# A transformer layer in emulated fp32: a fifth pair of k tiles in seven units, a fixed VectorE order at the start, and other banks for one projection

## The chip, the cores and the metric

The kernel runs on one core of one Trainium2 chip. The metric is the device time of one execution in microseconds (us). Engines: PE is TensorE (matmuls), DVE is VectorE, ACT is ScalarE, POOL is GpSimd, SP is SyncE, which here only issues DMAs.

## The reference

One layer on 256 tokens of 2048 channels. The parts that matter here are its matrix products with weights from HBM:

```python
z = u @ w_in                       # 2048 -> hq hf hi hg aq ak av, gates (2 x 2048)
o = hgrn2_scan(...)                # from hq, hf, hi; chunks of 64
ya = chunk_band_attention(...)     # from aq, ak, av
merged = gate_a * (y_a @ w_branch_a) + gate_b * (y_b @ w_branch_b)
h = h + merged @ w_out
h = h + square(relu(rms_norm(h) @ w_up)) @ w_down      # 2048 -> 8192 -> 2048
return rms_norm(h, norm_final_w)
```

All data are fp32.

## The kernel before, in words

**Three products for one.** Every fp32 operand is split into a high part, rounded to the matmul's faster format, and the rest. A split of weights is one cast on ACT (wh, L91) and one subtraction on DVE (wl, L92). A product is three matmuls: high by wh, high by wl, low by wh (L139, L140, L141 inside mm3). The activations (act_x, act_h, act_u) are split as they are made. A piece of weights is a raw tile of 128 x 1024: two k tiles of 128 rows by 512 columns. It is loaded by SP's queue (L215), and its two parts lie in the buffers wh and wl. There are four of each in the pool wpool, and from gb0 on a fifth one, which takes every fifth piece (buf, L201).

**The start.** After 12 warm-up matmuls (L81) the projections hf0 and hq0 run side by side, k tile by k tile, with x itself scaled and split on the way (L279 to L282; `xw` is x as loaded). They form their products transposed (L181 with wh, L186 with wl), two 256-token sums in a bank of their own each. Then hf1, then hq1. The banks of ps_acc are four; hf0 and hq0 hold them all, and add_parts (L195) adds their parts into f and zq.

**Units.** From av on, most products run as units of 256 tokens x 1024 columns x 16 k tiles. k tiles 0 to 3 and 4 to 7 with the two column halves make a 2 x 2 block matrix (A, B over D, C); it is multiplied in Strassen's way, in the form of Winograd, with 7 block products where 8 are usual. The sums of weights for it are formed in place: A += B and A += C on DVE (L846), B += C and D += A by accumulating DMAs that POOL issues (L851). The combinations of activations (S2, S4, S5, S7) are formed once per activation in combos. k tiles 8 to 15 are multiplied plainly. The block products are 11A, 22A, 12C, 11D, 21A, 21B, 21D, named after the bank they add to and the weight tile; each has two pieces of six matmuls a bank. A plain piece (`r` in the names) has two k tiles, 12 matmuls.

The order in a unit (run, L887): 11A; a late item of the unit before; 22A; another late item; 12C and 11D (11D first if there is no late item and the unit isn't spread); plain; 21A; plain; 21B; plain; plain; 21D; plain; plain; and the unit's own two last plain pieces are the late items of the next. "Spread" units are ga and gb; in them A += C comes after the subtractions of both 12C and 11D. All splits and sums have a raised priority; a scheduler puts each engine's instructions in order, and `issue_after` pins one behind another. Small work of the unit before (copies of y, L1211; gates, L729; evictions) is spread between the splits on ACT.

Units in order, with their start in us in the trace: av 245, qk 290, ga0 337, ga2 384, gb0 432, gb2 468, (branches by gemm2 514,) wo0 604, wo2 640, up00 683, up02 726, dn00 768, dn02 811, up10 852, up12 893, dn10 936, dn12 978, up20 1019, up22 1060, dn20 1103, dn22 1145, up30 1186, up32 1227, dn30 1270, dn32 1313 to 1359. upNM is columns of quarter N of the MLP's inner width, dnNM its way back.

**Loads.** The next unit's A is loaded during 21A, its B and C after 21B, its D after 21D, all on SP's queue, in the pools raw (6 tiles), rawd (2) and rawp (3).

Of the kernel before, what the change touches and what calls it, by code (L numbers as in the profile page):

```python
# [16 lines left out]
P = 128  # L17
# [33 lines left out]
def tile_hybrid_block(  # L51
# [26 lines left out]
    with tc.high_priority(offset=10000):  # L78
        nc.vector.memset(warm, 0.0)
        for _ in range(12):  # L80
            nc.tensor.matmul(ps_warm, warm, warm, start=True, stop=True)  # L81
# [6 lines left out]
    casts, marks, newest = [], [], []  # L88

    def split(hi, lo, src, copy=None):  # L90
        casts[:] = [(copy or nc.scalar.copy)(hi, src)]  # L91
        return nc.vector.tensor_tensor(lo, src, hi.bitcast(F32), op=ALU.subtract)  # L92
# [127 lines left out]
    def parts(raw, what):  # L220
# [9 lines left out]
        return [t.rearrange("p (a n) -> p a n", a=2) for t in made]  # L230

# [20 lines left out]
    def h2(what, bufs=10):  # L252
# [5 lines left out]
          weights(w_in_t, C_HQ, KD, T, "hq0", (1, 1) + (2,) * 7, beside=4)]  # L258
# [12 lines left out]
    for kt, n in zip(starts, steps):  # L271
# [3 lines left out]
        with tc.high_priority(offset=2000):  # L275
            for j in range(n):
# [3 lines left out]
                else:  # L280
                    nc.scalar.activation(hi, xw[:, j, :], AF.Copy, scale=g)
# [76 lines left out]
    acc_f1 = gemm_t(xT, w_in_t, C_HF + T, KD, "hf1")  # L358
# [376 lines left out]
    def combos(lhs, what, home, made, blocks=None):  # L735
# [11 lines left out]
        def final(i, s):  # L747
            t = home.tile([P, 4, 2, P], F32R, name=f"S{i}_{what}", tag=f"S{i}", bufs=1)
# [17 lines left out]

    def evict(dst, acc):
# [5 lines left out]

    class Unit:


        def __init__(self, lhs, S, w, n0, what, done, kt0=0, apart=NC, steps=lambda: (), start=5, fresh=None, held=False, tail=False):
# [4 lines left out]
            self.raw, self.dma, self.c, self.items, self.steps = {}, {}, {}, list(ITEMS), []  # L782

        def load(self, name):
# [3 lines left out]
                              for g in (0, 2)]  # L788

# [97 lines left out]
    def run(u, then=None):  # L887
# [18 lines left out]
        if not late and not u.spread:  # L906
# [24 lines left out]
        u.plain(1, (8, 9))  # L931
# [10 lines left out]
        u.plain(1, (10, 11))  # L942
# [15 lines left out]
        u.plain(0, (10, 11))  # L958
# [30 lines left out]
        late.append(lambda: u.plain(1, LATE[0]))  # L989
# [4 lines left out]
    for f in combos(xT, "x", tk, Sx):  # L994
# [50 lines left out]
    for m in range(NM):  # L1045
        scaled("k0", rstd, m, acc_k[m])
# [270 lines left out]
```

## Time and profile before

| | |
|---|---|
| median of 3 runs | 1369.27 us (1367.44 to 1372.15) |
| the profiled execution | 1368.19 us, span 1366.5 us |
| granted TensorE clock, mean | 0.999 |
| busy: PE, DVE, ACT, POOL | 99%, 82%, 69%, 11% of the span |
| DMA | 333.75 MB, mean 244 GB/s |

A line of the timeline gives start, duration, engine, line of the code, operation, tile written, tiles read, and in brackets the idle time of the engine before it with what released it. "PE acc_up10c" is a bank of unit up10, "wl_up10p11D" the low part for its product 11D, "wl_up10r" that of a plain piece. Matmuls overlap: one of 512 columns shows 0.39 us, and the next starts sooner. The durations below come from the one profiled execution.

### The profile page before, as it was taken

The numbers are of one execution on the slowest core, as the hardware profiler recorded it, in microseconds if no ns is written. First come the engines' busy times: TensorE is split into PE (matmuls) and PEld (weight loads), VectorE is DVE, ScalarE is ACT, GpSimd is POOL, SyncE is SP. The second block draws the span as 40 slices with busy tenths as digits, with TensorE's granted clock in tenths as the row PEclk, the third lists the DMA queues.
The fourth block names the chain that finished last, engine by engine and source line by source line (L and its number), as shares of the span: only waits on it lengthen the run. The fifth ranks groups of instructions, "written<-read, shape, count | busy, mean of one in ns | idle before, by whom it ended". The sixth has DMA issues, their size and how long they took to land.

```text
span 1366.5 us, 19044 instructions
## 1 busy us (share of the span) xinstructions
PE 1356.7 (99%) x6791; PEld 1123.1 (82%) x6791; DVE 1122.1 (82%) x1302; ACT 948.6 (69%) x1247; POOL 150.5 (11%) x231
## 2 busy tenths in 40 slices
PE   9999999999999999999999999999999999999997
PEld 7888888878778888888888888888888888888886
DVE  7888977887787775798998987789787888878886
ACT  6877765776777664455778766687666876668864
POOL 4000000111111000010121112100111002110210
PEclk9999999999999999999999999999999999999999
DMA  9754557788886986669899889988899888998892
GB/s 324 246 186 157 178 179 265 217 219 246 261 222 169 295 293 208 184 155 317 290 263 284 222 260 298 297 242 228 263 279 301 253 246 240 282 299 258 259 280 105
DMA packets 128895, 333.75 MB, mean 244 GB/s; under 512 B 11152, under 2 KB 12176, under 8 KB 128416
## 3 DMA queue, kind: packets, MB, share of 16 engines
q1 hardware_dynamic: 107936, 265.59, 56.4%
q0 software_dynamic: 20144, 66.14, 24.7%
q8 instruction: 53, 0.87, 0.3%
q10 hardware_dynamic: 720, 0.81, 0.2%
q14 instruction: 42, 0.34, 0.1%
HBM read 271.67 MB, written 10.49 MB: 206 GB/s over the span
## 4 chain that ended last, share of the span: by engine, by line
PE 98%; DMA 1%; ACT 0%; DVE 0%; issue 0%; SPq 0%; POOLq 0%; POOL 0%; ACTq 0%; DVEq 0%
PE acc_hf L181 2%; PE acc_hq L181 2%; PE tp_u L109 1%; PE acc_hg L139 1%; PE acc_qkc L139 1%; PE acc_hg L141 1%; PE acc_ba L141 1%; PE acc_hi L140 1%; PE acc_hi L139 1%; PE acc_bb L139 1%; PE acc_hi L141 1%; PE acc_hg L140 1%; PE acc_bb L141 1%; PE acc_ba L140 1%; PE acc_bb L140 1%; PE acc_ba L139 1%
## 5 line engine op out<-in xcount | busy, mean ns | idle before, releaser
L181 PE MATMUL acc_hf<-act_x,wh_hf 128*128 128x512 f32 x128 | 40.6, 399 | 0.4 <-DVE f L195 0.4
L181 PE MATMUL acc_hq<-act_x,wh_hq 128*128 128x512 f32 x128 | 40.5, 398 | 0.0
L91 ACT CAST wh_bb<-raw_bb 128x1024 fp32r<-128x1024 f32 x16 | 16.9, 1054 | 23.3 <-PE acc_ba L141 17.5
L92 DVE TENSOR_TENSOR wl_bb<-raw_bb,wh_bb 128x1024 fp32r<-128x1024 f32 x16 | 19.6, 1224 | 14.8 <-ACT wh_bb L91 14.7
L91 ACT CAST wh_ba<-raw_ba 128x1024 fp32r<-128x1024 f32 x16 | 16.8, 1053 | 19.9 <-PE acc_bb L141 13.8
L92 DVE TENSOR_TENSOR wl_ba<-raw_ba,wh_ba 128x1024 fp32r<-128x1024 f32 x16 | 19.6, 1223 | 10.8 <-ACT wh_ba L91 10.8
L186 PEld LDWEIGHTS acc_hq<-act_x,wl_hq 128*128 128x128 f32 x128 | 23.4, 188 | 6.1 <-DVE wl_hq L92 0.9
L186 PEld LDWEIGHTS acc_hf<-act_x,wl_hf 128*128 128x128 f32 x128 | 23.4, 188 | 6.0 <-DVE wl_hf L92 0.9
L1212 POOL DMA_DIRECT2D hd<-y x24 | 26.2, 1156 | 1.8 <-ACT y L1211 1.3
L92 DVE TENSOR_TENSOR wl_hf<-raw_hf,wh_hf 128x1024 fp32r<-128x1024 f32 (+2 forms) x21 | 20.3, 968 | 6.7 <-ACT wh_hf L91 6.7
L92 DVE TENSOR_TENSOR act_u<-tp_u,act_u 128x512 fp32r<-128x512 f32 x32 | 21.9, 685 | 4.7 <-ACT act_u L91 4.2
L139 PE MATMUL acc_bb<-wh_bb,act_yb 128*128 128x512 f32 x64 | 25.2, 393 | 0.0
L186 PE MATMUL acc_hq<-act_x,wl_hq 128*128 128x256 f32 x128 | 24.7, 280 | 0.4 <-DVE wl_hq L92 0.4
L186 PE MATMUL acc_hf<-act_x,wl_hf 128*128 128x256 f32 x128 | 24.7, 279 | 0.4 <-DVE wl_hf L92 0.4
L139 PE MATMUL acc_hg<-wh_hg,act_x 128*128 128x512 f32 x64 | 25.1, 392 | 0.0
L139 PE MATMUL acc_hi<-wh_hi,act_x 128*128 128x512 f32 x64 | 25.0, 391 | 0.0
L141 PE MATMUL acc_hg<-wh_hg,act_x 128*128 128x512 f32 x64 | 24.9, 390 | 0.0
L141 PE MATMUL acc_ba<-wh_ba,act_ya 128*128 128x512 f32 x64 | 24.9, 389 | 0.0
L141 PE MATMUL acc_hi<-wh_hi,act_x 128*128 128x512 f32 x64 | 24.9, 389 | 0.0
L140 PE MATMUL acc_hi<-wl_hi,act_x 128*128 128x512 f32 x64 | 24.9, 389 | 0.0
L140 PE MATMUL acc_hg<-wl_hg,act_x 128*128 128x512 f32 x64 | 24.9, 389 | 0.0
L139 PE MATMUL acc_ba<-wh_ba,act_ya 128*128 128x512 f32 x64 | 24.9, 389 | 0.0
(1996 smaller groups left out, 5226.6 us busy)
## 6 DMA issues: line engine op xcount, KB each, us to landing
raw_hi<-in_w_in_n_dram SPq DMA_DIRECT2D x16, 512.0 KB, 4.2
raw_hg<-in_w_in_n_dram SPq DMA_DIRECT2D x16, 512.0 KB, 4.3
raw_ba<-in_w_branch_a_dram SPq DMA_DIRECT2D x16, 512.0 KB, 4.6
raw_bb<-in_w_branch_b_dram SPq DMA_DIRECT2D x16, 512.0 KB, 4.7
raw_hf<-in_w_in_t_dram SPq DMA_DIRECT2D x12, 512.0 KB, 4.5
raw_hq<-in_w_in_t_dram SPq DMA_DIRECT2D x12, 512.0 KB, 5.5
hd<-y POOLq DMA_DIRECT2D x24, 256.0 KB, 7.4
raw_aq<-in_w_in_t_dram SPq DMA_DIRECT2D x8, 512.0 KB, 3.8
```

The source lines that it names most:

```text
L91: casts[:] = [(copy or nc.scalar.copy)(hi, src)]
L92: return nc.vector.tensor_tensor(lo, src, hi.bitcast(F32), op=ALU.subtract)
L109: nc.tensor.transpose(tp[:, j, :], src[:, j * P:(j + 1) * P], ident)
L139: nc.tensor.matmul(acc, hi, wh, start=first, stop=False, skip_group_check=True)
L140: nc.tensor.matmul(acc, hi, wl, start=False, stop=False, skip_group_check=True)
L141: newest[:] = [nc.tensor.matmul(acc, lo, wh, start=False, stop=last, skip_group_check=True)]
L181: newest[:] = [nc.tensor.matmul(acc[cb], wh[:, cb * P:(cb + 1) * P], r.rearrange("p u t -> p (u t)"), start=kt == 0, stop=last)]
L186: newest[:] = [nc.tensor.matmul(acc[cb][:, 0:T], wl[:, cb * P:(cb + 1) * P], r[:, 0, :], start=False, stop=False)]
L1212: nc.gpsimd.dma_start(hd[n][m], t, accum_op=ALU.add)
```

## The change

**A fifth pair.** Seven units (gb2, dn02, up10, dn12, up20, dn22, up30) also take k tile 8 with k tile 9 into the 7 products. Their weights are two more tiles, X (columns of A and D: k tile 8 is A's, 9 is D's) and Y (B's and C's), each with one buffer, loaded in the place of a plain piece each. Each product gets a third piece, a half: 512 columns, with its own cast, subtraction and buffer, and 3 matmuls. Four sums of 512 columns a unit are formed in X and Y on DVE (L862 in the new numbering). Two plain pieces go, and the unit has one late item instead of two. So the units behind a five unit have one late item in them; the rule for "11D first" is now "fewer than two late items", which holds in up10, up12 and so on. A += C is pinned behind the first of the two middle products. `fifths` forms the fifth part of the combinations of x (in gb0), h (in dn02) and u (in dn00, dn10, dn20).

**Room for it.** The fifth buffer of wh and wl is gone, everywhere. S7 is written into the place of one block of the activation that is never used otherwise; so the split of that block is left out for h and u. For x, which the plain projections read whole, S7 is formed only after ak.

**The start.** Ten warm-ups for 12; the DVE order is pinned; the third load of hq moves from ACT's queue to SP's; hf1's sums lie in the two banks of ps_sm.

By the printed order the matmul rows of PE go from 5997 to 5976, DVE's rows from 1278 to 1368, ACT's from 1169 to 1203.

The core of the diff:

```diff
-        for _ in range(12):
+        for _ in range(10):
...
-    def gemm_t(rhs, w, n0, nkt, what):
-        acc = new_acc(what)
+    def gemm_t(rhs, w, n0, nkt, what, acc=None):
+        acc = acc or new_acc(what)
...
-        if "fifth" in homes:
-            taken[tag] += 1
-        last = taken[tag] > 0 and taken[tag] % 5 == 0
-        return (homes["fifth"] if last else wpool).tile([P, 2 * NC], F32R, name=f"{tag}_{what}", tag=tag, bufs=1 if last else 4)
+        return wpool.tile([P, 2 * NC], F32R, name=f"{tag}_{what}", tag=tag, bufs=4)
...
+    def half(raw, a, what):
+        made = [buf(t, what)[:, 0:NC] for t in ("wh", "wl")]
+        with tc.high_priority(offset=2000):
+            lows.append(split(*[t.rearrange("p (c n) -> p c n", n=T) for t in made], view5(raw, a)))
+        return made
...
-          weights(w_in_t, C_HQ, KD, T, "hq0", (1, 1) + (2,) * 7, beside=4)]
+          weights(w_in_t, C_HQ, KD, T, "hq0", (1, 1) + (2,) * 7, beside=2)]
...
+            if kt in (1, 2):
+                es.enter_context(tc.issue_after(low[0].ins))
...
-    acc_f1 = gemm_t(xT, w_in_t, C_HF + T, KD, "hf1")
+    acc_f1 = gemm_t(xT, w_in_t, C_HF + T, KD, "hf1", [ps_sm.tile([P, NC], F32, name=f"acc_hf1{j}", tag="sm") for j in range(2)])
...
+    ITEMS5 = [(1, (10, 11)), (1, (12, 13)), (0, (10, 11)), (0, (12, 13)), (0, (14, 15)), (1, (14, 15))]
+    FIFTH = {"A": ("X", 0), "D": ("X", 1), "B": ("Y", 0), "C": ("Y", 1)}
+    SUMS5 = {("22", "A"): "B", ("21", "A"): "C", ("21", "B"): "C", ("21", "D"): "A"}
...
+                if not g and self.five and (i, name) in SUMS5:
+                    dst, src = [view5(self.raw[r], a) for r, a in (FIFTH[name], FIFTH[SUMS5[i, name]])]
+                    with tc.issue_after(lows[-1].ins), tc.high_priority(offset=2000):
+                        nc.vector.tensor_tensor(dst, dst, src, op=ALU.add)
...
+            if self.five:
+                raw, a = FIFTH[name]
+                mm3(self.c[i], *left(4), *half(self.raw[raw], a, f"{self.what}p{i}{name}5"), False, False)
...
-        if not late and not u.spread:
+        if len(late) < 2 and not u.spread:
             seconds.reverse()
...
         seconds[0]()
+        behind_first = lows[-1]
...
-            if u.spread:
-                es.enter_context(tc.issue_after(lows[-1].ins))
+            if u.spread or u.five:
+                es.enter_context(tc.issue_after((lows[-1] if u.spread else behind_first).ins))
             u.sums("A", "C")
...
             then.load("D")
+            then.load5("X")
...
-        late.append(lambda: u.plain(1, LATE[0]))
+        if not u.five:
+            late.append(lambda: u.plain(1, LATE[0]))
         late.append(rest)
```

**What moves on DVE at the start.** Before; act_x is the scaled x, lm and e are small vectors that are needed later:

```order
L279 TENSOR_SCALAR act_x_107<-xw_140,vt 128x256
L92 TENSOR_TENSOR wl_hf_0_122<-raw_hf_0_120,wh_hf_0_121 128x256
L282 SCALAR_TENSOR_TENSOR act_x_107<-xw_140,vt,act_x_107 128x256
L91 CAST wh_hf_0_121<-raw_hf_0_120 128x256
L307 TENSOR_TENSOR e_375<-vt,lm 128x8
L92 TENSOR_TENSOR wl_hf_0_122<-raw_hf_0_120,wh_hf_0_121 128x256
L92 TENSOR_TENSOR wl_hq_0_132<-raw_hq_0_130,wh_hq_0_131 128x256 x2
```

And after:

```order
L92 TENSOR_TENSOR wl_hf_0_120<-raw_hf_0_118,wh_hf_0_119 128x256
L92 TENSOR_TENSOR wl_hq_0_130<-raw_hq_0_128,wh_hq_0_129 128x256
L291 TENSOR_SCALAR act_x_105<-xw_138,vt 128x256
L294 SCALAR_TENSOR_TENSOR act_x_105<-xw_138,vt,act_x_105 128x256
L91 CAST wh_hf_0_119<-raw_hf_0_118 128x256
L92 TENSOR_TENSOR wl_hf_0_120<-raw_hf_0_118,wh_hf_0_119 128x256
L92 TENSOR_TENSOR wl_hq_0_130<-raw_hq_0_128,wh_hq_0_129 128x256
```

The low parts of the first pieces of hf and hq now come ahead of x's second k tile, and e has left this stretch.

**What moves on DVE in up10, from 22A to the first plain piece.** Before; `raw_up10A<-raw_up10A,raw_up10C` is A += C:

```order
L846 TENSOR_TENSOR raw_up10A_7831<-raw_up10A_7831,raw_up10C_7880 128x1024
L92 TENSOR_TENSOR wl_up10p22A_8044<-raw_up10A_7833,wh_up10p22A_8043 128x1024
L92 TENSOR_TENSOR wl_dn02r_14_8056<-rawp_dn02r_14_7901,wh_dn02r_14_8055 128x1024
L846 TENSOR_TENSOR raw_up10A_7833<-raw_up10A_7833,raw_up10C_7882 128x1024
L92 TENSOR_TENSOR wl_up10p12C_8080<-raw_up10C_7880,wh_up10p12C_8079 128x1024
L92 TENSOR_TENSOR wl_up10p12C_8090<-raw_up10C_7882,wh_up10p12C_8089 128x1024
L92 TENSOR_TENSOR wl_up10p11D_8100<-rawd_up10D_7939,wh_up10p11D_8099 128x1024
L92 TENSOR_TENSOR wl_up10p11D_8110<-rawd_up10D_7941,wh_up10p11D_8109 128x1024
L92 TENSOR_TENSOR wl_up10r_8_8124<-rawp_up10r_8_7975,wh_up10r_8_8123 128x1024
```

And after:

```order
L92 TENSOR_TENSOR wl_up10p11D_8161<-rawd_up10D_8019,wh_up10p11D_8160 128x1024
L92 TENSOR_TENSOR wl_up10p11D_8171<-rawd_up10D_8021,wh_up10p11D_8170 128x1024
L92 TENSOR_TENSOR wl_up10p11D_8181<-rawx_up10X,wh_up10p11D_8180 128x512
L898 TENSOR_TENSOR raw_up10A_7913<-raw_up10A_7913,raw_up10C_7968 128x1024
L92 TENSOR_TENSOR wl_up10p12C_8188<-raw_up10C_7968,wh_up10p12C_8187 128x1024
L92 TENSOR_TENSOR wl_up10p12C_8198<-raw_up10C_7970,wh_up10p12C_8197 128x1024
L92 TENSOR_TENSOR wl_up10p12C_8208<-rawy_up10Y,wh_up10p12C_8207 128x512
L898 TENSOR_TENSOR raw_up10A_7915<-raw_up10A_7915,raw_up10C_7970 128x1024
L92 TENSOR_TENSOR wl_up10r_10_8219<-rawp_up10r_10_8057,wh_up10r_10_8218 128x1024
```

11D now comes ahead of 12C, each has a half behind it, and the two sums of A stand between 11D and the first plain piece, where they stood among 22A's splits.

**What moves on SP's queue at the end of dn02.** After; X and Y are the new loads, and the plain pieces of up10 stand behind X:

```order
L211 DMA rawy_up10Y<-in_w_up_dram 128x2x512
L211 DMA rawp_dn02r_14_7871<-in_w_down_dram 128x1024
L211 DMA rawd_up10D_8019<-in_w_up_dram 128x2x512
L211 DMA rawd_up10D_8021<-in_w_up_dram 128x2x512
L211 DMA rawx_up10X<-in_w_up_dram 128x2x512
L211 DMA rawp_up10r_10_8057<-in_w_up_dram 128x2x512
```

The load of Y has come in behind C's, and X stands between D's two loads and those of the plain pieces.

More of the change, by code (lines that the diff above doesn't have):

```diff
@@ L930, in run @@
         u.step(next(at))
-        u.plain(1, (8, 9))
+        u.plain(1, (10, 11) if u.five else (8, 9))
         item(u)
@@ L941, in run @@
         u.step(next(at))
-        u.plain(1, (10, 11))
+        u.plain(1, (12, 13) if u.five else (10, 11))
         u.less("12", u1)
@@ L951, in run @@
             then.load("C")
+            then.load5("Y")
         u.step(next(at))
-        u.plain(0, (8, 9))
+        u.plain(0, (10, 11) if u.five else (8, 9))
         u.less("22", u2)
@@ L957, in run @@
         u.step(next(at))
-        u.plain(0, (10, 11))
+        if not u.five:
+            u.plain(0, (10, 11))
         u.residual("11")
@@ L987, in rest @@
             u.end(1)
-        late.append(lambda: u.plain(1, LATE[0]))
+        if not u.five:
+            late.append(lambda: u.plain(1, LATE[0]))
         late.append(rest)
     Sx = {}
-    for f in combos(xT, "x", tk, Sx):
+    x_sums = combos(xT, "x", tk, Sx)
+    for f in x_sums[:3]:
         f()
@@ L1046, in tile_hybrid_block @@
         scaled("k0", rstd, m, acc_k[m])
+    x_sums[3]()
     yb += [new_act(f"yb{g}") for g in range(2)]
@@ L1204, in tile_hybrid_block @@
             units.append(Unit(lambda: hT, lambda: Sh, w_up, qd * (FF // NQ) + c * NC, f"up{qd}{c}", done,
-                              steps=(lambda turns=turns: turns(0)) if c else (lambda: ()) if qd else (lambda: h_blocks(2)), start=3 if c else 0, held=not qd and not c))
+                              steps=(lambda turns=turns: turns(0)) if c else (lambda: ()) if qd else (lambda: h_blocks(2)), start=3 if c else 0, held=not qd and not c, five=qd > 0 and not c))
         def out_of(m, n, acc, c=slice(0, NC), last=last, qd=qd):
@@ L1267, in tile_hybrid_block @@
                               lambda m, n, acc, *c, n0=n0, out_of=out_of: out_of(m, n0 + n, acc, *c), kt0=qd * KD,
-                              steps=(lambda: ()) if n0 else (lambda turns=turns, last=last: turns(2) + [(3, finals)] * last),
-                              start=0, tail=last and n0 == 2))
+                              steps=(lambda qd=qd: [(99, lambda: fifths(hT, "h", sp, Sh))] * (not qd)) if n0 else (lambda turns=turns, last=last: turns(2) + [(3, finals)] * last),
+                              start=3 if n0 else 0, tail=last and n0 == 2, five=n0 == 2 and not last))
     for u, then in zip(units, units[1:] + [None]):
```

78 lines of the change are left out of this document (57 added, 21 removed).

## The prediction

> **What bounds the kernel now.** I read the page first: the busy times (part 1) and the chain of work that ended last (part 4).
>
> ```profile
> span 1366.5 us, 19044 instructions
> ...
> PE 1356.7 (99%) x6791; PEld 1123.1 (82%) x6791; DVE 1122.1 (82%) x1302; ACT 948.6 (69%) x1247; POOL 150.5 (11%) x231
> ...
> PE 98%; DMA 1%; ACT 0%; DVE 0%; issue 0%; SPq 0%; POOLq 0%; POOL 0%; ACTq 0%; DVEq 0%
> ```
>
> TensorE (PE) is busy 99% of the span and is 98% of the chain. So a matmul that goes is worth its own time, and any new wait of PE costs its own time. Next the waits of PE; the columns are total us, times, longest us.
>
> ```profile
> PE ps_warm L81 <- DVE warm L79: 1.1, 1, 1.1
> PE acc_hf L186 <- DVE wl_hf L92: 0.4, 1, 0.4
> PE acc_hq L186 <- DVE wl_hq L92: 0.4, 1, 0.4
> PE acc_hf L181 <- DVE f L195: 0.4, 1, 0.4
> ```
>
> These are all its waits, and all lie in the first 31 us. Three of the four are touched by the change; from there on PE never waits. The third view cuts the span at the units (gb2, up00, dn02, up10):
>
> ```profile
> core 0: us, PE busy (x) PEld busy (x) DVE busy (x) ACT busy (x) POOL busy (x), PEclk, DMA share, GB/s
> 467.80:513.80 46.00, 46.00 (x204) 38.09 (x203) 32.30 (x29) 30.29 (x34) 2.11 (x3) 1.00 0.85 268
> 682.90:725.60 42.70, 42.70 (x198) 35.35 (x197) 40.86 (x44) 31.22 (x41) 8.46 (x11) 1.00 0.93 276
> 811.10:851.90 40.80, 40.80 (x181) 33.80 (x180) 32.26 (x29) 26.96 (x30) 6.94 (x9) 1.00 0.98 283
> 851.90:892.70 40.80, 40.80 (x181) 33.79 (x180) 32.36 (x29) 27.60 (x31) 6.93 (x9) 1.00 1.00 284
> ```
>
> In up10 VectorE (DVE) works 32.4 of 40.8 us, in up00 already 40.9 of 42.7. The weights' DMA share in up10 is 1.00. So a unit has some 8 us of DVE to spare where the change adds work, and no DMA to spare.
>
> **What is removed: matmuls.** The timeline of PE gives the price of one.
>
> ```profile
> 857.35 0.39 PE L139 MATMUL acc_up10c<-wh_up10p22A,S_h 128*128 128x512 f32 x1
> ...
> 860.07 0.39 PE L139 MATMUL acc_dn02c<-wh_dn02r,act_u 128*128 128x512 f32 x1
> ```
>
> Between these two starts lie the 12 matmuls of product 22A: 2.72 us, 0.227 us each. A unit has 7 products x 4 tiles x 3 plus 8 plain k tiles x 4 x 3 = 180; with a fifth pair 7 x 5 x 3 + 6 x 4 x 3 = 177. Seven units lose 3 each: 21 x 0.227 = **4.77 us**. Nothing hides this, since PE is the chain.
>
> **The start.** PE, DVE and ScalarE (ACT) before:
>
> ```profile
> 1.12 4.77 PE L81 MATMUL ps_warm<-warm 128*128 128x128 f32 x24 [1.12 <-DVE warm L79]
> 5.65 0.71 PE L181 MATMUL acc_hf<-act_x,wh_hf 128*128 128x512 f32 x2
> 6.81 0.50 PE L186 MATMUL acc_hf<-act_x,wl_hf 128*128 128x256 f32 x2 [0.45 <-DVE wl_hf L92]
> ...
> 8.57 0.63 PE L181 MATMUL acc_hf<-act_x,wh_hf 128*128 128x512 f32 x2
> 9.04 0.40 PE L186 MATMUL acc_hf<-act_x,wl_hf 128*128 128x256 f32 x2
> ...
> 9.97 0.63 PE L181 MATMUL acc_hf<-act_x,wh_hf 128*128 128x512 f32 x2
> ```
> ```profile
> 5.83 0.55 DVE L279 TENSOR_SCALAR act_x<-xw,vt 128x256 fp32r<-128x256 f32 x1 [0.52 <-DMA xw<-in_x_t_dram]
> 6.31 0.45 DVE L92 TENSOR_TENSOR wl_hf<-raw_hf,wh_hf 128x256 fp32r<-128x256 f32 x1
> ...
> 9.31 0.69 DVE L92 TENSOR_TENSOR wl_hf<-raw_hf,wh_hf 128x512 fp32r<-128x512 f32 x1 [0.28 <-ACT wh_hf L91]
> ```
> ```profile
> 8.00 0.51 ACT L281 ACTIVATE act_x<-xw,vt 128x256 fp32r<-128x256 f32 x1 [1.56 <-DMA xw<-in_x_t_dram]
> 8.66 0.62 ACT L91 CAST wh_hf<-raw_hf 128x512 fp32r<-128x512 f32 x1
> ```
>
> DVE waits for a load of x (5.83) with wl_hf queued behind it (6.31), and PE waits for wl_hf. The new order puts wl_hf and wl_hq ahead. Both PE waits of 0.45 go, and two warm-ups fewer let the first real matmul come earlier. What is late next is k tile 2: its x comes from a DMA at 8.00, its cast ends at 9.28, and it starts at 9.97. So at most 9.97 - 9.28 = 0.69 us can come back, and at least nothing; the third hq load, moved from ACT's queue into SP's, stands ahead of later loads of x there and can take some 0.4 us (one issue, below). I take **0.4**, range -0.3 to 0.69. The Trainium skill ("TensorE: Matmul & The Clock Gate", Part 1: The HAM clock gate) says the array's clock opens only after a free-running window of about 3.4 us of activity, so ten warm-ups may end before it opens in some runs; an estimate by that page is up to 1 us of half-rate matmuls, which would turn this term into -0.6. No run here shows ten warm-ups; in the units shown above the granted clock was 1.00.
>
> **What is removed: the wait of hf1.**
>
> ```profile
> 29.01 0.63 PE L181 MATMUL acc_hq<-act_x,wh_hq 128*128 128x512 f32 x2
> 30.05 0.83 PE L181 MATMUL acc_hf<-act_x,wh_hf 128*128 128x512 f32 x2 [0.41 <-DVE f L195]
> ```
> ```profile
> 28.44 1.23 DVE L92 TENSOR_TENSOR wl_hf<-raw_hf,wh_hf 128x1024 fp32r<-128x1024 f32 x1 [0.69 <-ACT wh_hf L91]
> 29.58 0.75 DVE L195 TENSOR_TENSOR f<-acc_hf,f 128x256 f32<-128x256 f32 x2
> ```
>
> hf1 waits until the sums of hf0 have left their banks (f, L195). In other banks it need not. After a pair of such matmuls the next group starts 0.47 us on (8.57 to 9.04 above), so hf1 could start at 29.48: 0.57 us earlier. Its first pair also lasts 0.83 where others last 0.63. I take 0.57 and some 0.12 of the latter, **0.69** (0.57 to 0.77). The split at 28.44 is already hf1's second, so its first piece is ready, and nothing is late next: f is wanted again only when hf1's banks have taken all its pieces. So the gains are 4.77 + 0.4 + 0.69 = **5.86 us**.
>
> **What is added: splits and sums on DVE and ACT, with one buffer fewer.** Prices:
>
> ```profile
> L92 DVE TENSOR_TENSOR wl_up10r<-rawp_up10r,wh_up10r 128x1024 fp32r<-128x1024 f32 x7 | 8.6, 1224 | 4.2 <-ACT wh_up10r L91 3.9
> ```
> ```profile
> 478.96 2.36 DVE L846 TENSOR_TENSOR raw_gb2A<-raw_gb2A,raw_gb2C 128x1024 f32<-128x1024 f32 x2
> 481.23 1.22 DVE L92 TENSOR_TENSOR wl_gb2r<-rawp_gb2r,wh_gb2r 128x1024 fp32r<-128x1024 f32 x1
> ```
>
> A 1024-column operation lasts 1.22 us on DVE and follows the one before after 1.14 (2.27 for two); a 512-column one lasts 0.69 (9.31 above), in a row, by the same difference, some 0.6. Per unit two plain splits go (-2.4) and seven half splits and four sums of 512 come (+7.5): 32.4 + 5.1 = 37.5 of 40.1 us. ACT gains seven casts of 0.62 and loses two of 1.05: 27.6 + 2.2 = 29.8. On the average both still fit under PE. dn02 also forms h's fifth combinations (two operations of 512, four of 128 columns; about 2 us by these rows, less than 2.8): some 39.5 of 40.1. What decides is how far splits may run ahead. There were five buffers for wh and wl, now there are four, and a half piece fills one too. A split may start when the piece four places before it has been used. The av unit before gb0 already has four:
>
> ```profile
> 249.07 0.39 PE L139 MATMUL acc_avc<-wh_avp22A,S_x 128*128 128x512 f32 x1
> ```
> ```profile
> 249.35 1.05 ACT L91 CAST wh_avp12C<-raw_avC 128x1024 fp32r<-128x1024 f32 x1
> ```
>
> PE leaves the first 22A piece at 249.07, and the cast four places on starts 0.28 later. The subtraction starts 1.08 after its cast and lasts 1.22:
>
> ```profile
> 857.59 1.05 ACT L91 CAST wh_up10p12C<-raw_up10C 128x1024 fp32r<-128x1024 f32 x1 [1.23 <-issue]
> ```
> ```profile
> 858.67 1.22 DVE L92 TENSOR_TENSOR wl_up10p12C<-raw_up10C,wh_up10p12C 128x1024 fp32r<-128x1024 f32 x1 [0.36 <-ACT wh_up10p12C L91]
> ```
>
> That is 2.6 us from release to use. Three pieces in hand are 4.08 us of PE when full, but two full ones and a half are 3.40, plus 0.23 to the first matmul that reads wl: 1.0 us of slack, if DVE is free at that moment. A sum of 1.14 ahead of the split takes it all.
>
> **up10, up20, up30.** PE's order (pieces of 1.36, halves 0.68, late piece 2.72): 11A to 3.40, late 6.12, 22A 9.52, 11D 12.92, 12C 16.32, then the first plain piece. 11D's first buffer is released at 6.12, ACT has there two copies of y:
>
> ```profile
> 861.75 0.59 ACT L1211 COPY y<-acc_dn02c 128x512 f32<-128x512 f32 x1
> ```
>
> I put its cast at 6.85 and its subtraction at 7.93. From there DVE has 11D (1.14 + 1.14 + 0.60), a sum of A (1.14), 12C (2.28 + 0.60), a sum of A (1.14) and the plain split (1.22): 9.26, to 17.19. PE wants that at 16.32 + 0.23 = 16.55. So PE waits about 0.65; without the copies ahead 0, with the first copy at the release 1.4. Queued behind the late split on DVE is product 21A, whose slack is the plain piece's 2.72. 3 x 0.65 = **1.95** (0 to 4.3).
>
> **gb2** has both sums in a row ahead of the plain split, and two late pieces: 12C begins at 12.24, 11D at 15.64, plain at 19.04. 11D's buffer comes free at 12.24, behind a gate on ACT
>
> ```profile
> 478.91 0.69 ACT L729 ACTIVATE gate_gb<-acc_gb0c,rstd 128x512 f32<-128x512 f32 x1 [0.54 <-PE acc_gb0c L141]
> ```
>
> so its subtraction begins near 14.1, and 2.28 + 0.60 + 2.28 + 1.22 = 6.4 later, at 20.5, the plain piece is ready; PE wants it at 19.27: **1.25** (0.5 to 1.8).
>
> **up00** and others without a fifth pair lose only a buffer. up00's DVE has 1.8 us of air; one skipped split of h gives 1.2 back. I take **0.3** (0 to 0.9). dn02, dn12, dn22 have two late pieces, so their splits have 2.72 us more to catch up: 0 (to 0.5 each).
>
> **The X load.** X has one buffer. Where two five units follow each other (dn02 to up10, and so on, three times), X of the second loads only when the half split of 21D of the first has read it, some 6.1 us of PE plus up to 1 of slack before the next unit: -6.7. On SP's queue it stands where D stood, with the plain pieces' loads behind it.
>
> ```profile
> 838.13 1.74 SPq L215 DMA_DIRECT2D rawd_up10D<-in_w_up_dram  x2
> ```
> ```profile
> DMA to landing us min/median/max: 6.1/6.6/9.8
> ```
>
> With the median it lands at -6.7 + 0.4 + 6.6 = +0.3. X's cast, then two copies of y, then the late piece's split are in line on ACT; by the same durations they need X at -0.3. 0.6 us late is partly covered by other slack: 0.2 each, **0.6** in all.
>
> **Sum.** Waits 1.95 + 1.25 + 0.3 + 0.6 = 4.1; gains 5.86. Net -1.8: 1368.2 - 1.8 = 1366.4 against the profiled execution's 1368.19 (span 1366.5). The median of the runs is 1369.27, 1.1 above it, so 1367.5 there; I round to **1367.4**.
>
> **Rivals.** *A, four buffers are enough.* ACT's small copies fall elsewhere, splits start at release, and no unit waits. For it: av runs so without a wait of PE. Against: av has no half pieces. Then -5.86: 1363.4. Chance 0.33. *B, X comes late, slower.* The load of X takes as long as the longest of D's, 9.8: X lands at +3.5 instead of -0.3, in three units, 3.8 x 3 = 11.4 in place of 0.6: 1369.3 - 5.9 + 3.5 + 11.4 = 1378.3. Each us of landing over 6.0 costs one; the sign turns at (5.86 - 3.5)/3 = 0.8 per unit, a landing of 6.8 with nothing covered, and 4.1 us of loss is passed at 2.2, a landing of 8.2. For it: DMA share 1.00 in up10, and D's row. Against: the longest was the second of two loads in line. Chance 0.11. *C, the saving is given back nearly whole:* every wait above at its upper end, and one of 0.5 in each dn unit: 4.3 + 1.8 + 0.9 + 1.5 = 8.5, less 5.86, +2.6: 1371.9, no measurable change. Then DVE (37.5 of 40.1) sets the pace of the units and the matmuls saved are idle time. Chance 0.12. The forecast has 0.44.
>
> **How the numbers follow.** A measurement can tell 0.3%, 4.1 us, from no change. Faster by that: A (0.33) and 0.05 of the forecast, when its waits stay under 1.7. Slower: B's greater part (0.09) and 0.02 of C. The rest is the same: 0.51. The range holds A's value with 0.6 below, at 1362.8, and reaches up to 1370.8, 3.4 above the forecast, which takes in the upper ends of its waits in the up units (4.3 for 1.95) and in gb2 (1.8 for 1.25) and half of C. Outside are B (0.11), the other half of C (0.06) and 0.03 below.
>
> **What would show it.** PE's matmul records go down by 21. Each five unit is 0.68 shorter, where it doesn't wait. The waits of PE lose f L195 and wl_hf, and gain wl_gb2r and wl_up10r, wl_up20r, wl_up30r from DVE of 0.5 to 1.3 each, first plain piece. If no such wait is there, A holds; if PE or ACT waits for rawx of up10 over 1 us, B. Wrong would be: waits in dn02, dn12, dn22 or in units without a fifth pair over 1 us each, or k tile 2 later than 9.97.

## The result and the profile after

| | before | changed |
|---|---|---|
| median of 6 runs, us | 1368.92 | 1377.47 |
| lowest to highest | 1367.44 to 1372.15 | 1374.34 to 1379.95 |
| profiled execution, span | 1368.19, 1366.5 | 1378.76, 1377.1 |
| ratio, 95% interval | | 1.0060 (1.0049 to 1.0072) |

The change makes the kernel 8.6 us slower. The forecast was 1367.4, and the range ended at 1370.8. It is rival B's side and size (1378.3). Three executions at a far lower granted clock (one of no_five, one of best2, one of the kernel before) are left out of the medians below.

The waits of PE in the changed kernel, longest first:

```profile
PE acc_ga2c L140 <- ACT u_ga L849: 1.4, 1, 1.4
PE acc_dn30c L140 <- ACT u_dn L849: 1.3, 1, 1.3
PE ps_warm L81 <- DVE warm L79: 1.1, 1, 1.1
PE acc_up20c L140 <- ACT wh_up20p11A L91: 0.8, 1, 0.8
PE acc_dn02c L141 <- DVE wl_dn02r L92: 0.8, 1, 0.8
PE acc_dn22c L141 <- DVE wl_dn22r L92: 0.8, 1, 0.8
PE acc_gb2c L141 <- DVE wl_gb2r L92: 0.6, 1, 0.6
PE acc_dn12c L141 <- DVE wl_dn12r L92: 0.5, 1, 0.5
PE acc_dn12c L140 <- ACT wh_dn12r L91: 0.5, 1, 0.5
PE acc_gb0c L140 <- ACT acc_gb0c L849: 0.4, 1, 0.4
```

Before, PE waited only at the start. Now the late pieces of dn02, dn12 and dn22 are late, each in the unit behind it: up10, up20, up30. The waits of ACT for DMAs say why:

```profile
ACT wh_up20p11A L91 <- DMA rawx_up20X<-in_w_up_dram: 7.0, 1, 7.0
ACT wh_up30p11A L91 <- DMA rawx_up30X<-in_w_up_dram: 4.9, 1, 4.9
ACT wh_up10p11A L91 <- DMA rawx_up10X<-in_w_up_dram: 4.8, 1, 4.8
```

ACT stands still 5 to 7 us for X, with everything behind it. The load of up20's X (issue in us; then us to landing), and ACT at its place:

```profile
L211 SPq DMA_DIRECT2D rawx_up20X<-in_w_up_dram x1: 840/840/840, 1016.9 to 1016.9; - x1
...
DMA to landing us min/median/max: 11.0/11.0/11.0
```
```profile
1019.10 2.01 ACT L91 CAST wh_up20p11A<-raw_up20A 128x1024 fp32r<-128x1024 f32 x2 [0.26 <-PE acc_dn12c L142]
1028.07 0.62 ACT L91 CAST wh_up20p11A<-rawx_up20X 128x512 fp32r<-128x512 f32 x1 [6.97 <-DMA rawx_up20X<-in_w_up_dram]
1028.60 1.07 ACT L1274 COPY y<-acc_dn12c 128x512 f32<-128x512 f32 x2
1029.55 1.06 ACT L91 CAST wh_dn12r<-rawp_dn12r 128x1024 fp32r<-128x1024 f32 x1
```

up20 starts on PE at 1025.0, so X lands 2.9 us into the unit. Behind its cast come the two copies of y and the late piece dn12r. In up10 the load took 8.8 us and landed 0.7 into the unit, in up30 8.9 and 0.8. PE from there on, and the windows with the granted clock:

```profile
1027.51 0.39 PE L142 MATMUL acc_up20c<-wh_up20p11A,act_h 128*128 128x512 f32 x1
1028.74 0.50 PE L140 MATMUL acc_up20c<-wh_up20p11A,act_h 128*128 128x512 f32 x1 [0.84 <-ACT wh_up20p11A L91]
1029.47 0.50 PE L141 MATMUL acc_up20c<-wl_up20p11A,act_h 128*128 128x512 f32 x1 [0.23 <-DVE wl_up20p11A L92]
...
1030.66 0.79 PE L140 MATMUL acc_dn12c<-wh_dn12r,act_u 128*128 128x512 f32 x1 [0.46 <-ACT wh_dn12r L91]
1031.92 0.79 PE L141 MATMUL acc_dn12c<-wl_dn12r,act_u 128*128 128x512 f32 x1 [0.47 <-DVE wl_dn12r L92]
...
1033.37 0.63 PE L141 MATMUL acc_dn12c<-wl_dn12r,act_u 128*128 128x512 f32 x1
1033.79 0.63 PE L142 MATMUL acc_dn12c<-wh_dn12r,act_u 128*128 128x512 f32 x1
```
```profile
1029.00:1031.00 2.00, 1.32 (x4) 0.59 (x3) 1.91 (x3) 2.00 (x4) 1.01 (x2) 0.89 0.97 143
1031.00:1034.00 3.00, 2.54 (x6) 1.69 (x6) 3.00 (x4) 2.29 (x4) 1.58 (x2) 0.50 0.89 164
1034.00:1037.00 3.00, 3.00 (x8) 2.32 (x8) 1.34 (x2) 0.90 (x2) 0.37 (x1) 0.50 1.02 216
1037.00:1040.00 3.00, 3.00 (x13) 2.44 (x13) 1.42 (x2) 2.58 (x3) 1.34 (x2) 0.93 1.09 225
```

In the third of four waits the granted clock falls to 0.50. By the clock's means in these windows it falls near 1030.6 and is back near 1037.4, after some 6.8 us. Matmuls start 0.42 us apart there (1033.37 to 1033.79) where 0.227 is usual. That is some 3.4 us more. This fall belongs to the profiled execution, whose mean clock is 0.996. The other five have 0.998 or 0.999, like the kernel before, so they can't hold a fall of that length; what they lose in its place is in no trace.

To see where all the time went, I took the starts of all matmuls of a trace and summed by unit what their distance exceeds the usual one (0.227 for 512 columns). A matmul counts for the unit whose tiles it reads, so a late piece counts for its own unit. Us lost, in four profiled executions; the last two are experiments below:

| | before | changed | four_buffers | split_x |
|---|---|---|---|---|
| up to av | 8.6 | 8.4 | 9.4 | 8.2 |
| ga2 | 2.8 | 4.8 | 2.8 | 2.9 |
| gb0, gb2 | 0.0 | 2.4 | 1.6 | 1.9 |
| wo0, wo2, up00 | 0.9 | 1.7 | 2.5 | 3.3 |
| dn02, up10 | 0.0 | 1.4 | 1.6 | 0.2 |
| dn12, up20 | 0.0 | 6.0 | 2.0 | 0.3 |
| dn22, up30 | 0.0 | 1.5 | 3.1 | 0.3 |
| dn30 | 0.4 | 1.9 | 4.7 | 2.1 |
| whole kernel | 21.8 | 36.8 | 36.6 | 27.8 |

The changed kernel loses 15.0 us more than before, and saves 4.8 of matmuls: 10.2 of the 10.6 by which the spans differ. Nine of the 15 lie where X is late, and 3.4 of these nine are the low clock in up20. The profile of four_buffers is that of its slowest execution (1383.36, median 1380.14).

### The profile page after: what moved, and what is told of

Read it like the earlier page. It is cut to its first block, busy times and chain, and to the rows that moved or that the text cites. A ratio compares the mean times of both kernels' runs of the same rounds, so it can differ in the third digit from the quotient of the medians.

```text
span 1377.1 us, 19148 instructions
## 1 busy us (share of the span) xinstructions
PE 1360.3 (99%) x6766; PEld 1119.9 (81%) x6766; DVE 1153.8 (84%) x1390; ACT 963.3 (70%) x1282; POOL 150.8 (11%) x231
## 4 chain that ended last, share of the span: by engine, by line
PE 63%; DVE 2%; issue 2%; DMA 2%; ACT 1%; POOL 0%; POOLq 0%; ACTq 0%; DVEq 0%
PE acc_ba L142 1%; PE acc_bb L140 1%; PE acc_bb L142 1%; PE acc_ba L141 1%; PE acc_bb L141 1%; PE acc_ba L140 1%; PE acc_wo2c L142 1%; PE acc_wo2c L140 1%; PE acc_dn32c L142 1%; PE acc_dn00c L140 1%; PE acc_dn20c L140 1%; PE acc_dn22c L141 1%; PE acc_dn10c L140 1%; PE acc_dn32c L140 1%; PE acc_up12c L142 1%
## 5 line engine op out<-in xcount | busy, mean ns | idle before, releaser
L1275 POOL DMA_DIRECT2D hd<-y x24 | 22.5, 962 | 52.5 <-ACT y L1274 48.1
L140 PE MATMUL acc_bb<-wh_bb,act_yb 128*128 128x512 f32 x64 | 25.2, 393 | 0.0
L141 PE MATMUL acc_ba<-wl_ba,act_ya 128*128 128x512 f32 x64 | 24.9, 389 | 0.0
L141 PE MATMUL acc_bb<-wl_bb,act_yb 128*128 128x512 f32 x64 | 24.9, 389 | 0.0
L142 PE MATMUL acc_bb<-wh_bb,act_yb 128*128 128x512 f32 x64 | 24.9, 389 | 0.0
```

What stands on the lines that cost most here:

```text
L140: nc.tensor.matmul(acc, hi, wh, start=first, stop=False, skip_group_check=True)
L141: nc.tensor.matmul(acc, hi, wl, start=False, stop=False, skip_group_check=True)
L142: newest[:] = [nc.tensor.matmul(acc, lo, wh, start=False, stop=last, skip_group_check=True)]
L1275: nc.gpsimd.dma_start(hd[n][m], t, accum_op=ALU.add)
```

## The experiments

Theory X: the late load of X in the three up units is most of the loss. Rival B here: the lost fifth buffer is. ("Rival B" in the expectations means this one.) All ratios are against the kernel before on the same chip.

**Four buffers alone (four_buffers)**, the kernel before with `buf` as in the change:

```diff
-        return (homes["fifth"] if last else wpool).tile([P, 2 * NC], F32R, name=f"{tag}_{what}", tag=tag, bufs=1 if last else 4)
+        return wpool.tile([P, 2 * NC], F32R, name=f"{tag}_{what}", tag=tag, bufs=4)
```

> The kernel before with four buffers of wh and wl everywhere and nothing else changed. Theory X (most of the loss is the late load of X in up10, up20 and up30): the lost buffer alone costs only the waits that the profile after shows in units without a fifth pair and that need no late DMA of X: gb0 0.7, up00 0.6, wo0 0.2, dn30 1.5, together 3.0 us; ratio about 1.002. Rival B (the lost buffer is what costs: splits can no longer run ahead): 8 us or more, ratio 1.006 or above. No theory expects it to be faster.

Measured: 1380.14, ratio 1.0084 (1.0071 to 1.0097), 11.8 us slower. Theory X's 3.0 was wrong, and rival B's 8 or more came out. The waits of PE:

```profile
PE acc_dn30c L139 <- ACT u_dn L801: 2.4, 1, 2.4
...
PE acc_up10c L140 <- DVE wl_up10r L92: 0.9, 2, 0.7
PE acc_up00c L140 <- DVE wl_up00r L92: 0.9, 1, 0.9
PE acc_dn22c L140 <- DVE wl_dn22r L92: 0.8, 1, 0.8
```

They are spread. By the matmuls' starts gb0, gb2, up00, up10, dn12, up20, dn22 and up30 lose 0.7 to 1.9 us each, all but gb0 waiting for a plain piece's subtraction, and dn30 loses 4.3. By the table a unit with the fifth pair (split_x's up10: 0.2) bears four buffers better than one without (1.5 here).

**The start alone (start_only)**, all start edits put into the kernel before.

> The kernel before with the start edits alone (ten warm-ups, DVE order pinned, the third hq load on SP's queue, hf1's sums in other banks). The prediction put 1.1 us of gain on it. By the profile after, hf1 gives back 0.75 and the rest of the start loses 0.15, because the low part of x's k tile 3 stands ahead of wl_hf of k tile 2 on DVE: 0.6 us of gain. Theory X: ratio 0.9995, no change that can be measured. A rival by which the start edits shift loads and cost something later (the bias of the attention landed 1.5 us later in ga2): up to 2 us slower, 1.0015.

Measured: 1368.90, ratio 1.0005 (0.9996 to 1.0013). The edits together bring nothing.

**No two five units in a row (up_only)**:

```diff
-  start=3 if n0 else 0, tail=last and n0 == 2, five=n0 == 2 and not last))
+  start=3 if n0 else 0, tail=last and n0 == 2, five=False))
```

> The changed kernel with the fifth pair in gb2, up10, up20 and up30 only, so that no unit with a fifth pair follows another and X's buffer is free long before its load. It keeps four buffers, the start and the order 11D before 12C only where one late item is left. Theory X: ACT no longer waits for X in up10, up20, up30; 9 matmuls come back (2.0 us), the waits of dn02, dn12, dn22's late pieces go (7 us in the median of after): about 5 us faster than the changed kernel, 3 to 4 us slower than before, ratio 1.0025. Rival B: the waits stay, only the matmuls come back: 1379, ratio 1.0075.

Measured: 1375.93, ratio 1.0047 (1.0035 to 1.0059). In its profiled execution (1372.6) up10, up20, up30 and dn02 lose 0.0, as theory X has it, though X is still one tile with one buffer and the sums are formed in the same order. dn12 and dn22, which have no fifth pair here, lose 0.8 each. The median is 4 us above what was expected; the other executions lie at 1372.8 and at 1375.6 to 1377.0, and what the slower ones lose isn't in the trace.

**X in two tiles (split_x)**: A's half of X gets its own tile and is released earlier:

```diff
-    SUMS5 = {("22", "A"): "B", ("21", "A"): "C", ("21", "B"): "C", ("21", "D"): "A"}
+    SUMS5 = {("22", "A"): ["AB"], ("21", "A"): ["AC"], ("21", "B"): ["BC", "DA"]}
...
+            then.load5("XA")
             then.load5("Y")
...
-            then.load5("X")
+            then.load5("XD")
```

> The changed kernel with X in two tiles of 512 columns, one for A and one for D, and D += A formed at 21B instead of 21D: A's tile is free some 10 us earlier and its load is issued with Y's. All seven units keep the fifth pair. Theory X: the waits of ACT for X go in the three units, and with them some 7 us: 1370 to 1371, ratio 1.001. Rival B: the splits are late anyway because of the buffers, at most 1 us comes back: 1376, ratio 1.005.

Measured: 1370.56, ratio 1.0017 (1.0009 to 1.0026): 6.9 us less than the changed kernel by the medians and 5.9 by the two ratios, as theory X said. The three rows of the table in which X was late fall from 8.9 to 0.8. The edit changes three things at once: the tile, the time of its load and the place of the sum D += A. The waits that are left:

```profile
PE acc_dn30c L140 <- ACT u_dn L851: 1.4, 1, 1.4
...
PE acc_gb2c L141 <- DVE wl_gb2r L92: 0.6, 1, 0.6
PE acc_wo2c L141 <- DVE wl_wo2r L92: 0.6, 1, 0.6
PE acc_up00c L141 <- DVE wl_up00p22A L92: 0.5, 1, 0.5
```

**The load put back (split_old)**: split_x with `load5("XA")` behind D's loads again.

> split_x with the load of A's tile of X put back to X's old place, behind D's loads at 21D, while the two tiles and the early D += A stay. It tells whether split_x won by the time of that load or by the other order of the sums. Theory X (the load is late): ACT waits for XA again in up10, up20 and up30, and most of split_x's 7 us is gone: 1375 to 1378, ratio 1.006. Rival: the order of the sums was what helped: 1370.6, ratio 1.0016. In between: the tile is free 10 us earlier, so its load waits only for SP's queue; if the loads of D ahead of it are what is late, the wait is as long as with one tile.

Measured: 1370.59, ratio 1.0016 (1.0007 to 1.0025). It didn't do what it was meant to: since the tile was free, the scheduler issued its load ahead of D's all the same.

```profile
L211 SPq DMA_DIRECT2D rawxa_up10XA<-in_w_up_dram x1: 577/577/577, 845.3 to 845.3; - x1
...
DMA to landing us min/median/max: 7.0/7.0/7.0
```

It lands at 852.3, 6.2 us ahead of the unit's start (858.5). So it doesn't tell the load from the sums. up_only does, in its profile: the sums are as in the change, X is loaded long before (up20's at 888.9), and the waits for X are gone.

**No fifth pair (no_five)**: `five=False` in all units of the changed kernel.

> The changed kernel with the fifth pair in no unit: four buffers, S7 in its new place, the start edits and the order rule stay, the matmuls are those of before. Theory now: the lost fifth buffer costs about 12 us in the old order of a unit (the run with four buffers alone), and the fifth pair's own order of work (one late item, 11D before 12C, the sum of A behind the first middle product) needs fewer buffers. Then without the fifth pair the loss of the buffer shows whole: 1378 to 1381, ratio 1.008, slower than the changed kernel in spite of X. Rival: the fifth pair itself is the load, and without it four buffers with S7's saved splits do nearly as well as before: 1371 to 1374, ratio 1.003.

Measured: 1381.33, ratio 1.0091 (1.0076 to 1.0106). As the theory says: without the pair the four buffers cost their whole price. With it and X in time (split_x) the kernel is 10.8 us faster than this one, while 21 matmuls are 4.8. That the pair's order of work needs fewer buffers is shown for part of the rest only: between the two profiles the rows dn02 to up30 of the table above differ by 3.7 us, and dn30 by 4.4, where PE waits for u_dn and the clock falls behind it:

```profile
PE acc_dn30c L140 <- ACT u_dn L849: 3.1, 1, 3.1
```

**dn30.** Three tries at its wait. In the changed kernel the load of wf (the final norm's weights) stands on POOL's queue behind D += A, which waits for 11D's subtraction:

```profile
1292.99 0.85 POOL L903 DMA_DIRECT2D rawd_dn30D<-raw_dn30A  x1 [1.97 <-DVE wl_dn30p11D L92]
1293.53 0.88 POOL L1321 DMA_DIRECT2D wf<-in_norm_final_w_dram  x1
```
```profile
1304.11 1.91 ACT L1322 ACTIVATE wf<-wf 128x2048 f32<-128x2048 f32 x1 [1.81 <-DMA wf<-in_norm_final_w_dram]
1305.93 0.57 ACT L849 COPY u_dn<-acc_dn30c 128x512 f32<-128x512 f32 x1
```

The load takes 10.6 us, ACT waits for it, and the copy u_dn for which PE waits stands behind. split_wf moves the load to SP's queue (`nc.sync.dma_start(fin["w"], ...)`):

> X in two tiles as in split_x, and the load of the final norm's weights (wf) issued from SP's queue instead of POOL's, where it stood behind D += A of dn30, which waits for 11D's split. By the profiles of after and split_x PE waits 1.4 us in dn30 for the copy u_dn, which stands behind the scaling of wf on ACT, which waits for that load. Theory: the wait goes, 1.5 us less than split_x: 1369, ratio 1.0005. Rival: the scaling itself (1.9 us on ACT) holds the copy back, and nothing changes: 1370.6, ratio 1.0017.

Measured: 1378.99, ratio 1.0070 (1.0058 to 1.0082), both wrong. On ACT the scaling stands where it stood in split_x, behind 21B's second cast. But SP's queue issued the load at 1289.1 where POOL's had issued it at 1284.5, and it took 12.5 us where it had taken 10.7. So it landed 6.4 us later and the wait grew, with the clock at half from within it on (the reason that split_late's expectation gives below, an earlier place of the scaling, does not hold):

```profile
PE acc_dn30c L140 <- ACT u_dn L851: 7.3, 1, 7.3
```

split_late leaves the load and pins the scaling behind 21D's last cast:

```diff
+        def scale_w():
+            with tc.issue_after(casts[0].ins):
+                nc.scalar.activation(fin["w"], fin["w"], AF.Copy, scale=D ** 0.5)
```

> split_x (X in two tiles) with the scaling of wf on ACT put behind the last split of dn30's 21D; the load stays on POOL's queue. In split_x PE waited 1.4 us in dn30 for the copy u_dn behind that scaling; with the load on SP's queue the scheduler put the scaling further ahead and PE waited 7.3. Theory: the wait in dn30 goes whole: 1370.6 - 1.6 = 1369.0, ratio 1.0004. Rival: another wait takes its place in dn30, since four buffers hold the splits back there: 1370.5, ratio 1.0016.

Measured: 1370.72, ratio 1.0020 (1.0011 to 1.0029): the rival. The wait for u_dn is gone and another stands in its place. dn30 loses 2.0 where it lost 2.1, and dn32 0.6 where it lost nothing:

```profile
PE acc_dn30c L141 <- DVE wl_dn30r L92: 1.1, 2, 0.8
```

The same scaling in the kernel before with four buffers (four_late) and in up_only (up_late):

> The kernel before with four buffers and the scaling of wf put behind 21D's split in dn30. In the profile of four_buffers dn30 lost 4.3 us (2.4 of waiting for u_dn, the rest at half the TensorE clock), the units gb0 to dn22 some 10 together. Theory: dn30's part goes, the rest stays: 1380.1 - 4.5 = 1375.6, ratio 1.0052. Rival: the buffers' cost lies in dn30 nearly whole: 1370, ratio 1.001.

Measured: 1379.52, ratio 1.0087 (1.0071 to 1.0104). dn30 falls from 4.7 to 1.9 in the profiles, but the median only by 0.6: neither number came out. In the profile of four_late, its median execution, the table's other rows lose much what they lose in four_buffers (8.5 us more than before from gb0 to up30, there 10.0), so most of the price of the buffer lies in them.

> up_only (fifth pair in gb2, up10, up20, up30) with the scaling of wf put behind 21D's split in dn30. up_only's times lay in two groups, 1372.6 to 1372.8 and 1375.6 to 1377.0; its profile was one of the first group. Theory: the second group is executions in which the wait in dn30 lasts longer and the TensorE clock falls to half for some us, so it goes: 1371, all in one group, ratio 1.002. Rival: the second group comes from somewhere else, and both groups only move down by 1.5: median 1374.5, ratio 1.0045.

Measured: 1374.21, ratio 1.0044 (1.0032 to 1.0057): the rival.

**hf1's banks alone (hf1_banks)**, the kernel before with only that edit.

> The kernel before with hf1's sums in the banks of ps_sm and nothing else. The start edits together gave nothing that can be measured (ratio 1.0005); by the profile of after hf1 gives back 0.75 us. Theory: the other start edits take it away again, so hf1 alone is 0.7 us faster than before, ratio 0.9995. Rival: hf1's wait is only moved to a later place: 0, ratio 1.000.

Measured: 1367.72, ratio 0.9992 (0.9983 to 1.0001), 0.6 less in the medians: as the theory says, but the interval just holds 1.

**The repairs together (best_try, best2).** best_try is X in two tiles, wf on SP's queue, the start of before but for hf1's banks, and in gb2:

```diff
-                es.enter_context(tc.issue_after((lows[-1] if u.spread else behind_first).ins))
+                es.enter_context(tc.issue_after((lows[-1] if u.spread and not u.five else behind_first).ins))
```

> X in two tiles, wf loaded from SP's queue, the start of before except for hf1's banks, and in gb2 the two sums A += C put behind 12C's split instead of 11D's. By the profiles: split_x 1370.6, less 1.5 for dn30, less 0.7 for the start, less 0.8 for gb2's first plain piece: 1367.6, ratio 0.9995. Rival: the waits taken away here come back as later ones of the same four buffers: 1370, ratio 1.001.

Measured: 1375.50, ratio 1.0049 (1.0036 to 1.0061), spoilt by wf as split_wf was (PE waits 6.2 us for u_dn). gb2 fell from 1.1 to 0.2 lost. best2 has the late scaling instead:

> X in two tiles, the scaling of wf put late, hf1's sums in other banks with the rest of the start as before, and gb2's sums A += C behind 12C's split. From split_x 1370.6: less 1.6 (dn30), less 0.8 (start), less 0.9 (gb2, as in the profile of best_try): 1367.3, ratio 0.999, about as fast as hf1's banks alone (1367.7). Rival: the parts don't add up, since the four buffers leave no slack: 1369, ratio 1.0005.

Measured: 1368.73, ratio 1.0003 (0.9994 to 1.0012): the rival's number. No version beats the kernel before by more than can be told.

**What a wait of PE costs (stall9, stall18)**: the kernel before with 9 or 18 needless copies on ACT in up20, and 22A's casts pinned behind them.

```diff
+                for _ in range(9):
+                    held = nc.scalar.copy(junk, u.c["11"][:, 0:160])
```

> The kernel before with one delay: in up20, nine needless copies of 160 columns on ACT ahead of the casts of 22A, pinned behind the first product. They take some 2.2 us, and PE should wait about 1.5 to 2 us once. Theory (a short wait of PE costs only itself): 1368.4 + 2 = 1370.4, ratio 1.0015, clock 1.00 throughout. Rival (any wait of PE makes the clock fall): 3.5 us more, 1374, ratio 1.004.

Measured: 1371.21, ratio 1.0023 (1.0012 to 1.0033); one wait of 1.5 us, some 24 us behind the copies (1048.3 to 1049.8, for ACT in a plain piece of up20), clock 1.00 throughout. The theory's clock came out and its price nearly: 2.8 us in the medians, and as much lost between matmuls, where the one listed wait explains 1.5 to 1.7 and many small gaps the rest.

> The same with eighteen copies, some 4.5 us, so that PE waits about 4 us in up20. Theory: behind a wait of this length the granted clock is 0.50 for some us, as in up20 of the changed kernel (3.4 us lost there) and in dn30 of split_wf: 4 + 3.4 us, 1376, ratio 1.0055. Rival (the low clock in those profiles has another cause, heat or load, and not the wait): only the wait itself, 1372.4, ratio 1.003.

Measured: 1374.98, ratio 1.0045 (1.0031 to 1.0059): nearer to the theory, since the clock did fall, for some 3.4 us. Three executions have a mean clock of 0.997 and 1374.3 to 1375.8; the fourth has 0.998 and 1372.47. Its waits and windows:

```profile
PE acc_up20c L140 <- ACT wh_up20p22A L92: 2.3, 1, 2.3
...
PE acc_up20c L141 <- DVE wl_up20p22A L93: 0.8, 1, 0.8
```
```profile
1027.00:1030.00 3.00, 1.25 (x6) 0.71 (x4) 0.00 (x0) 2.87 (x9) 0.24 (x1) 1.00 1.09 243
1030.00:1033.00 3.00, 1.71 (x4) 1.15 (x5) 2.49 (x3) 3.00 (x5) 1.41 (x2) 0.84 0.87 152
1033.00:1036.00 3.00, 3.00 (x9) 2.38 (x8) 3.00 (x3) 1.84 (x2) 0.06 (x1) 0.59 0.81 107
```

The clock falls behind waits of 3.1 us within 4. How much it takes isn't told by the sum of the waits alone: 1.5 in one piece here (stall9) and 1.4 in dn30 of split_x went without a fall, and in up20 of the change 0.84, 0.23 and 0.46, also 1.5 in all, went with one. By the starts the last is the longest: 2.2 us lost within 3.2, and only three matmuls begun in between, against 1.7 and 1.6 in one piece in the other two.

## Why the prediction was wrong

**The step that failed is the X load**, priced 0.2 us a unit, 0.6 in all. It measured 5.9 to 6.9 (split_x against the changed kernel). The mechanism was described rightly, also its point of decision: "they need X at -0.3". What failed is the landing time, and with it the allowance for "other slack". The row from which the time was taken, 6.1/6.6/9.8, mixes the two loads of D with POOL's two accumulating DMAs into the same tile. The loads alone, from the same view with the window 836 to 842:

```profile
L215 SPq DMA_DIRECT2D rawd_up10D<-in_w_up_dram x2: 378/378/379, 838.1 to 839.5; - x2
...
DMA to landing us min/median/max: 6.1/6.1/6.1
```

So neither 6.6 nor rival B's 9.8 is the time of a load, and "the longest was the second of two loads in line" is a misreading: it is one of POOL's.

In the changed kernel X was issued 8.1 us ahead of its unit, earlier than the -6.7 of the sum, and took 8.8, 11.0 and 8.9. It isn't X alone: D's loads just ahead of it took 8.4 to 10.9. The time goes with the number of loads still under way. In these rows of 512 KB loads each lands some 1.3 us behind the one before (D at 855.6 and 856.9), in the trace of before as well (D at 844.2 and 845.6). When X of up10 was issued six loads were under way, so it was the seventh, and 7 x 1.3 = 9.1 is near its 8.8. X of up20 was the eighth and took 11.0; D of up10 in the trace of before was the fifth and took 6.1. This is read from the traces, and no run varies it alone. The prediction passed over this row of loads, to which the change adds that of Y.

X landed at +0.7 and +0.8 in two units, which by the prediction's own rule costs 1.0 and 1.1: the late pieces of dn02 and dn22 lost 1.0 and 1.0. Nothing of it was covered by "other slack". The prediction's sign for B came too: ACT waited 4.8 us for X of up10. In up20, at +2.9, the rule gives 3.2, and 6.0 were lost: 2.6 in waits and the rest at the low clock. That rival B's 1378.3 lies so near to 1377.47 is luck: it has 3.8 in each of three units, where the trace has 1.4, 6.0 and 1.5, and its time of landing comes from a DMA of another kind. By the prediction's own numbers X was 0.6 late in each unit; taking two thirds of that away, and giving X a chance of 0.11 to come later still, was the error of judgment.

**The lost buffer was priced too low, and in part at the wrong place.** The first plain piece of up10, up20 and up30 was put at 0.65 each; in split_x, where X is in time, these units lose 0.25 each, and no wait for wl_up10r, wl_up20r or wl_up30r is listed in the change or in split_x. gb2's 1.25 measured 1.1 to 1.7, and up00's 0.3 measured 0.6 in the change and 1.4 in split_x. Not in the sum at all were dn30 (1.5), gb0 (0.7) and wo0 (0.2): units which the change doesn't touch but whose splits ran ahead on the fifth buffer. "and others without a fifth pair lose only a buffer" is where they were passed over. For the kernel before, that buffer alone is worth 11.8 us. The sum had 4.1 us of waits, and the profile of the change shows 15.0. With X repaired the time (1370.56) lies inside the range, 3.2 above the forecast; by the table most of that lies in units that lost only the buffer (gb0, wo2, up00, dn30).

**The matmuls** were right: PE's records go from 6791 to 6766, 25 fewer, of which four are the two warm-ups. Their price, 4.8 us, is worked out and was not measured alone, but it fits: from the start of dn12 to that of dn20 split_x takes 123.5 us and the kernel before 124.4, and split_x loses 0.4 more between matmuls there, so the two units with the pair save 0.7 each. **hf1** was right: the next start came 0.47 us after the last pair,

```profile
29.18 0.63 PE L182 MATMUL acc_hq<-act_x,wh_hq 128*128 128x512 f32 x2
29.65 0.62 PE L182 MATMUL acc_hf<-act_x,wh_hf 128*128 128x512 f32 x2
```

and hf1_banks gained 0.6 for 0.69. **The rest of the start** brought nothing for 0.4. The first real matmul came no earlier (5.65 in both), and with ten warm-ups its pair lasted 1.15 us where it had lasted 0.71:

```profile
5.65 1.15 PE L182 MATMUL acc_hf<-act_x,wh_hf 128*128 128x512 f32 x2
```

This fits the half rate of which the prediction warned, at about 0.4 us. It isn't in every execution: in up_only and split_x, also with ten, the pair lasts 0.71 and 0.73, and in hf1_banks, with twelve, 1.02. The two waits of 0.45 went, but k tile 2 lost what they gave: its first pair came at 9.40 (before at 9.97), its first matmul with wl_hf only at 10.95 (before at 10.44). On DVE:

```profile
9.80 0.48 DVE L294 SCALAR_TENSOR_TENSOR act_x<-xw,vt,act_x 128x256 fp32r<-128x256 f32 x1 [0.86 <-ACT act_x L293]
10.20 0.68 DVE L92 TENSOR_TENSOR wl_hf<-raw_hf,wh_hf 128x512 fp32r<-128x512 f32 x1
```

In the new order the low part of x's k tile 3 stands ahead of wl_hf of k tile 2 and waits 0.86 for ACT. Before, wl_hf stood first, at 9.31. The prediction passed over this pair of rows of the new order.

**ga2** lost 2.0 more in the one profiled execution of the change, and 0.1 in split_x: the attention's bias took 6.2 us to land there and 4.6 before, and DVE waited 2.2 us for it and 0.2 before. Its cause is open.

**The clock** in the units wasn't among the terms. The Trainium skill ("TensorE: Matmul & The Clock Gate", Part 1: The HAM clock gate) says that the clock falls to half after an idle window of about 3.4 us. The runs agree with the half. They differ in what sets it off: in up20 of the change PE was not idle through any such window, it ran three matmuls between the first three of its waits, and in stall18 its longest wait was 2.3 us.

What stays open: why up_only's executions lie in two groups, what the changed kernel loses in the executions whose clock didn't fall, which of split_x's three changes gave its gain, beyond what the one profile of up_only tells, why split_x loses 0.9 more in wo2 and 0.8 more in up00 than the change does, and ga2.

## What to carry to other kernels

A buffer that is taken away is paid for by every unit that ran ahead on it, also those the change leaves alone: look at each unit's slack, not only at the changed ones. A single-buffered load whose tile is read to the end of one unit and wanted at the start of the next lands late when the queue is full. Price it by the loads still under way when it is issued, each times the distance between landings (here 1.3 us for 512 KB), and not by the median of one tile's row; look first which DMAs that row holds. Here ACT worked in the order of its queue, so a late load cost everything behind the instruction that waited for it: 7.0 us of ACT in up20, with two copies and a late piece behind.

## What the runs showed of the hardware that was not expected

- Short waits of PE close together halved the granted clock, with matmuls between them: 2.2 us lost within 3.2 in up20 of the change and 3.5 within 4 in stall18; 1.7 and 1.6 lost in one piece (stall9, dn30 of split_x) didn't. The clock stayed at 0.50 for 6.8 us in the change, 3.4 in stall18 and, from within the wait of 7.3 in dn30 of split_wf, some 10. In up20 of the change this cost some 3.4 us on top of the waits.
- In a row of 512 KB loads each landed some 1.3 us behind the one before, so a load took 6.1 us as the fifth under way (before), 8.8 as the seventh and 11.0 as the eighth (the change). Size told less: the load of wf, 1024 KB in its tile, took 10.2 us before, and loads of 512 KB issued next to it 11.0 to 12.6 in the median.
